# Out-projection by seven block products, with the fox gates last and the GLA output grouped by rows

## The chip, the cores and the metric

One core of one Trainium2 chip. The kernel's time is the device time in microseconds (us) of one launch; a time that is given is the median of several runs. Engines: TensorE (PE in the profile) multiplies matrices, VectorE (DVE), ScalarE (ACT) and GpSimd (POOL) work on elements, SyncE (SP) only issues transfers (DMAs). Each engine runs its own queue in order, and semaphores hold an instruction until what it needs is there.

## The reference

One layer of a decoder trunk over 16 meta tokens and 512 tokens, width D = 2048, in float32. Three token mixers run on disjoint heads of 128: gated DeltaNet (6 heads), GLA (5), forgetting attention, here "fox" (5). Together they give the 16 x 128 = 2048 columns of `o`. Cut to what matters:

```python
proj = rms_norm(x, norm_w) @ w_in                          # all projections, 8 k columns
o_dn  = gated_head_norm(gated_delta_rule_chunked(...), dz, dn_norm_w)   # norm, then * silu(dz)
o_gla = gated_head_norm(gla_chunked(...), gz, gla_norm_w)
o_fox = forgetting_attention(...) * silu(fz)
o = concatenate([o_dn, o_gla, o_fox], -1)[:, PAD:]         # 512 x 2048
out = rms_norm(x + o @ w_out, final_norm_w)                # w_out: 2048 x 2048
```

In one GLA chunk the output is `o = (q*exp(g)) @ S + attn @ v`, and in fox it is `softmax(q @ k.T + c_t - c_s) @ v`.

## The kernel before

**Precision.** A float32 operand of a large product is split into `hi` (a copy on ScalarE in TensorE's fp32r format) and `lo` (the rest, a subtract on VectorE); a product is three matmuls, hi x hi, hi x lo and lo x hi (`split`, L144/L145).

**Stages.** Activations lie with channels on the 128 partitions and tokens along the row. `inproj` (its matmuls are L168, tiles `pp`) makes one block of 128 projected channels from 16 k-blocks x 3 terms = 48 matmuls over 512 tokens; blocks are numbered, and pp42, 46, 50, 54 and 58 are the five fox gates `fz`. Weights come in halves of 512 KB (`load_half`). The order of work is DeltaNet in two groups of three heads, the GLA gates, three GLA pairs (`gla_pair`, two heads of 64 key rows each in one tile), five fox heads (`fox_head`), the out-projection. A planner orders the instructions of each engine from the order of the program, its own costs of instructions, and priorities; weight splits stand in a block of high priority.

**Gates.** `gate_z` projects a gate block, multiplies it by the row norm on VectorE (L299), and `silu` builds z / (1 + exp(-z)) by one GpSimd maximum (L287), three ScalarE functions (L288 and the two lines after it) and one VectorE multiply. For DeltaNet and GLA the gate lies in a tile of the pool `zp` (11 tiles) and the head's output is multiplied into it. In `fox_head` the gate is made inside the head, ahead of its softmax, and the output product `pfo` is multiplied by it when it leaves PSUM.

**GLA output.** L769 adds the attention part, a matmul over 128 rows, and L770 the state part over 64 rows: one head of a pair is in rows 0 to 63 and the other in 64 to 127. The two lines alternate, block after block and head after head.

**Out-projection.** `split_o` splits the 16 head outputs (L905/L906). For each of four 512-wide column chunks, four PSUM banks `pa` (four groups of 128 tokens) gather k-blocks 0 to 13, 3 terms each (L913, in `mms`). Chunks 0 to 2 are then added to the tokens (L949). K-blocks 14 and 15 (LAST = 14) are held back for the end: their weights `wl` are split early, and at the end one tile `pz` after another is made from them (L913) and added (L972), squared with a sum (L974), and multiplied by the norm weight on GpSimd (L976). When a group of tokens has its four chunks, the norm is taken (L978 to L980), the tiles are scaled (L984, L986, L988) and written (L990). The matmuls of chunk 0 need the heads that are done, not the last fox head, so the planner puts them between the steps of that head.

PSUM has eight banks: four of `psb` (projections, `pa`) and four of `psm`. A ring of seven rows of 531 elements (`row`) serves gates, softmax rows, and squares.

Of the kernel before, what the change touches and what calls it, by code (L numbers as in the profile page):

```python
# [8 lines left out]
F32 = mybir.dt.float32  # L9
# [9 lines left out]
P = 128  # L19
# [58 lines left out]
def tile_hybrid_trunk(ctx, tc, xT, xtok, mtok, w_gate, w_in, w_out, consts, lmask, fin_w, out, dbg=None):  # L78
# [5 lines left out]
    hp = pool("hp", 2 * KT)  # L84
    wp = pool("wp", 2)
    zp = pool("zp", 11)
    six = pool("six", 8)
    wk = pool("wk", 2)
# [4 lines left out]
    def row(name, dt=F32):  # L93
        return wk.tile([P, 3 + T], dt, tag="row", bufs=7, name=name)
# [198 lines left out]
    zs = {}  # L293

    def gate_z(kind, h, t=None):
        parts = inproj((kind, h), meta=False)
        p_, t0, n = parts[0]
        z = row(f"z{kind}{h}")[:, :T]
        V.tensor_tensor(out=z[:, :S], in0=p_, in1=rstd[:, t0 : t0 + n], op=ALU.mult)  # L299
# [339 lines left out]
    def gla_pair(p):  # L639
# [125 lines left out]
        for e in range(ne):  # L765
            rr = slice(64 * e, 64 * e + 64)
            for b in range(NB):
                bs = slice(b * P, (b + 1) * P)
                PE.matmul(po[e][:, bs], at[:, e * NB + b, :], vt[:, e, bs], start=True, stop=False)  # L769
                PE.matmul(po[e][:, bs], qd[rr, bs], ss[b][rr, :], start=False, stop=True)  # L770
# [17 lines left out]
    def fox_head(h):  # L788
# [22 lines left out]
        cc = six.tile([P, 2 * T + S], F32, tag="six", name=f"fc{h}")  # L811
        z = wk.tile([P, S], F32, tag="gd", name=f"fz{h}") if h < 2 else cc[:, T + S : T + 2 * S]
        gate_z("fz", h, z)
# [53 lines left out]
        V.tensor_tensor(out=z, in0=po[:, :512], in1=z, op=ALU.mult)  # L867


    for g in range(2):  # L870
        for h in range(max(NF, H * g), H * g + H):
            gate_z("dz", h)
        st = dn_keys(g)
        dn_values(g, st)
        dn_queries(g, st)
        dn_inverse(g, st)
        dn_mix(g, st)
    for h in range(GLA_HEADS):
        gate_z("gz", h)
# [8 lines left out]
    for p in range(3):  # L888
        gla_pair(p)
    for h in range(GLA_HEADS):  # L890
        dump(f"ogl{h}", zs["gz", h])
    for h in range(FOX_HEADS):
        fox_head(h)
    for h in range(FOX_HEADS):
        dump(f"ofx{h}", zs["fz", h])


    heads = [("dz", h) for h in range(DN_HEADS)] + [("gz", h) for h in range(GLA_HEADS)] \
        + [("fz", h) for h in range(FOX_HEADS)]
    oparts = []  # L900

    def split_o(i):
        z = zs[heads[i]]
        hi, lo = part(f"oh{i}"), part(f"ol{i}")
        A.copy(hi, z)  # L905
        V.tensor_tensor(out=lo, in0=z, in1=hi.bitcast(F32), op=ALU.subtract)  # L906
        oparts.append((hi, lo))

    def mms(p_, hi, lo, i, tb, first, last):
        s = slice(tb * P, (tb + 1) * P)  # L910
        oh, ol = oparts[i]
        for n, (o_, w_) in enumerate(((oh, hi), (oh, lo), (ol, hi))):
            PE.matmul(p_, o_[:, s], w_, start=(first and n == 0), stop=(last and n == 2))  # L913

    LAST = 14
    halves = lambda w: [[t[:, j * 512 : (j + 1) * 512] for t in w] for j in range(2)]
    acc, wl = {}, {}

    def load_last(c):
        raw = wp.tile([P, 1024], F32, tag="raw", name=f"rawl{c}")  # L920
        nc.sync.dma_start(out=raw, in_=w_out[c, LAST // 2])
        r = []
        for j in range(2):
            hi, lo = part(f"wlh{c}{j}"), part(f"wll{c}{j}")
            split(raw[:, j * 512 : (j + 1) * 512], hi, lo)
            r.append((hi, lo))
        return r

    for i in range(LAST):
        split_o(i)  # L930
    for cc in range(4):
        pa = [psb.tile([P, 512], F32, tag="b", name=f"pa{cc}{tb}") for tb in range(4)]
        for kp in range(LAST // 2):
            w = halves(load_half(w_out[cc, kp], f"o{cc}_{kp}"))
            for j in range(2):
                i = 2 * kp + j
                for tb in range(4):
                    mms(pa[tb], *w[j], i, tb, i == 0, cc < 3 and i == LAST - 1)
            if cc == 3 and kp % 2 and kp < 6:
                c = kp // 2  # L940
                wl[c] = load_last(c)
        for tb in range(4):
            if 4 * cc + tb < 11:
                a = zp.tile([P, S], F32, tag="zs", name=f"acc{cc}{tb}")
            else:
                a = six.tile([P, S], F32, tag="six", name=f"acc{cc}{tb}")
            nc.scalar.dma_start(out=a, in_=xtok[tb * P : (tb + 1) * P, cc * 512 : (cc + 1) * 512])
            if cc < 3:
                V.tensor_tensor(out=a, in0=a, in1=pa[tb], op=ALU.add)  # L949
            acc[tb, cc] = a  # L950
        if cc == 0:
            for i in range(LAST, KT):
                split_o(i)
    wl[3] = halves(load_half(w_out[3, LAST // 2], "l3"))
    fw = []
    for c in range(4):
        f = part(f"fw{c}").bitcast(F32)
        nc.scalar.dma_start(out=f, in_=fin_w[c * 512 : (c + 1) * 512].partition_broadcast(P))
        fw.append(f)
    ss = wk.tile([P, 4, 5], F32, tag="fss", bufs=1, name="fss")  # L960
    rr = wk.tile([P, 4], F32, tag="frs", bufs=1, name="frs")
    for tb in range(4):
        for cc in (3, 0, 1, 2):
            a = acc[tb, cc]
            cuts = 2 if (tb, cc) == (3, 2) else 1
            for n in range(cuts):
                c = slice(512 // cuts * n, 512 // cuts * (n + 1))
                p_ = pa[tb] if cc == 3 else psm.tile([P, 512], F32, tag="m", name=f"pz{tb}{cc}{n}")
                for j in range(2):
                    hi, lo = wl[cc][j]  # L970
                    mms(p_[:, c], hi[:, c], lo[:, c], LAST + j, tb, cc < 3 and j == 0, j == 1)
                V.tensor_tensor(out=a[:, c], in0=a[:, c], in1=p_[:, c], op=ALU.add)  # L972
                sq = row(f"sqf{tb}{cc}{n}")
                A.activation(sq[:, c], a[:, c], AF.Square, accum_out=ss[:, tb, cc + 2 * n : cc + 2 * n + 1])  # L974
            if cc != 2:
                G.tensor_tensor(out=a, in0=a, in1=fw[cc], op=ALU.mult)  # L976
        r = rr[:, tb : tb + 1]
        V.reduce_sum(r, ss[:, tb, : 3 + cuts], axis=mybir.AxisListType.X)  # L978
        A.activation(r, r, AF.Ln, scale=1.0 / D, bias=eps_c)
        A.activation(r, r, AF.Exp, scale=-0.5)  # L980
        for cc in (3, 0, 1, 2):
            a = acc[tb, cc]
            if cc == 0:
                A.activation(a, a, AF.Copy, scale=r)  # L984
            elif cc == 2:
                V.scalar_tensor_tensor(out=a, in0=a, scalar=r, in1=fw[cc], op0=ALU.mult, op1=ALU.mult)  # L986
            else:
                V.tensor_scalar_mul(a, a, r)  # L988
            q = nc.scalar if cc % 2 else nc.sync
            q.dma_start(out=out[tb * P : (tb + 1) * P, cc * 512 : (cc + 1) * 512], in_=a)  # L990
# [55 lines left out]
```

## Time and profile before

| what | value |
|---|---|
| median of 3 runs | 1048.95 us (1047.97 to 1050.61) |
| profiled execution | 1048.64 us, span 1046.9 us |
| mean granted TensorE clock | 0.991 |
| busy: PE, DVE, ACT, POOL | 1019.8, 574.8, 410.7, 134.9 us |
| L168, three groups of 1456 matmuls | 378.5, 376.8, 376.2 us |
| L913, three groups of 224 matmuls | 88.0, 87.9, 79.1 us |
| bytes moved | 105.15 MB, mean 100 GB/s |

A group row of the profile reads: line, engine, operation, output and input tiles, shapes, count, then busy time, mean ns of one, and the idle time before it with what ended that. Busy times of matmuls overlap in the pipeline, so the time of one is read from a window: its length over its count. A timeline row has start and length in us, then the same names; in brackets stands the wait ahead of it.

### The profile page before, as it was taken

Reading aid. Unit: us, or ns where it says so; the run is one execution under the profiler, and the core shown is the slowest. Engines: PE = TensorE matmul, PEld = TensorE weight load, DVE = VectorE, ACT = ScalarE, POOL = GpSimd, SP = SyncE. Lnnn points to the kernel's source line nnn. Section 1 sums busy time; section 2 is a strip of 40 time slices with the busy share of each in tenths; the row PEclk is TensorE's granted clock in tenths of the full one; section 3 lists DMA queues with packets and bytes.
Section 4 is the critical chain, followed back from the end, with each engine's and each line's share of the span. In section 5 each row is a group of like instructions: output and inputs, shape, how many; then the busy total and the mean of one; then the engine's idle time right before and its main releaser. Section 6 shows DMA issues by size and latency. Waiting matters only on the chain.

```text
span 1046.9 us, 19027 instructions
## 1 busy us (share of the span) xinstructions
PE 1019.8 (97%) x7787; PEld 914.5 (87%) x7787; DVE 574.8 (55%) x1251; ACT 410.7 (39%) x895; POOL 134.9 (13%) x137
## 2 busy tenths in 40 slices
PE   9999999999999999999999999999999999999994
PEld 7899999989999888899989878898989888888883
DVE  6366868855567972334828274455444474332437
ACT  6643533343455333244344443333323262222234
POOL 0021312220213131000100010110101010000014
PEclk9999999999999998999999999999999999999998
DMA  9613222223222322222212122222222263222424
GB/s 351 233 48 127 82 89 92 99 77 108 89 69 82 96 102 77 69 77 73 78 42 67 46 87 74 94 72 86 89 84 87 86 204 126 93 82 100 141 81 160
DMA packets 42347, 105.15 MB, mean 100 GB/s; under 512 B 10589, under 2 KB 13917, under 8 KB 42260
## 3 DMA queue, kind: packets, MB, share of 16 engines
q1 hardware_dynamic: 26848, 90.23, 24.6%
q10 hardware_dynamic: 15412, 13.70, 4.5%
q8 instruction: 61, 1.00, 0.4%
q14 instruction: 26, 0.21, 0.1%
HBM read 98.74 MB, written 5.05 MB: 99 GB/s over the span
## 4 chain that ended last, share of the span: by engine, by line
PE 54%; DVE 3%; ACT 1%; issue 1%; DMA 0%; DVEq 0%
PE pp L168 29%; PE pa L913 15%; PE pss L708 1%; PE pgo L770 1%; PE pfo L863 1%; PE pgo L769 1%; PE pfa L831 1%; PE pz L913 1%; DVE acc L988 1%; PE pfx L846 1%; ACT sqf L974 0%; PE pfd L832 0%; PE pfo L866 0%; DVE acc L986 0%; PE pgk L660 0%
## 5 line engine op out<-in xcount | busy, mean ns | idle before, releaser
L168 PE MATMUL pp<-xh,whi 128*128 128x264 f32 (+2 forms) x1456 | 378.5, 312 | 0.9 <-DVE vg L278 0.8
L168 PE MATMUL pp<-xh,wlo 128*128 128x264 f32 (+2 forms) x1456 | 376.8, 311 | 0.0
L168 PE MATMUL pp<-xl,whi 128*128 128x264 f32 (+2 forms) x1456 | 376.2, 310 | 0.0
L168 PEld LDWEIGHTS pp<-xh,whi 128*128 128x128 f32 x1456 | 244.5, 190 | 16.0 <-issue 1.4
L168 PEld LDWEIGHTS pp<-xl,whi 128*128 128x128 f32 x1456 | 245.2, 190 | 14.4 <-issue 1.4
L168 PEld LDWEIGHTS pp<-xh,wlo 128*128 128x128 f32 x1456 | 245.4, 190 | 13.3 <-issue 0.3
L145 DVE TENSOR_TENSOR wlo<-raw,whi 128x1024 fp32r<-128x1024 f32 x110 | 136.4, 1240 | 124.6 <-ACT whi L144 123.8
L144 ACT CAST whi<-raw 128x1024 fp32r<-128x1024 f32 x110 | 115.3, 1049 | 202.2 <-PE pp L168 181.1
L913 PE MATMUL pa<-whio,ol 128*128 128x512 f32 x224 | 88.0, 393 | 0.0
L913 PE MATMUL pa<-wloo,oh 128*128 128x512 f32 x224 | 87.9, 393 | 0.0
L913 PE MATMUL pa<-whio,oh 128*128 128x512 f32 x224 | 79.1, 396 | 0.0
L145 DVE TENSOR_TENSOR wloo<-rawo,whio 128x1024 fp32r<-128x1024 f32 x28 | 34.6, 1236 | 75.2 <-ACT whio L144 75.1
L144 ACT CAST whio<-rawo 128x1024 fp32r<-128x1024 f32 x28 | 29.4, 1049 | 93.7 <-PE pa L913 60.1
L913 PEld LDWEIGHTS pa<-whio,ol 128*128 128x128 f32 x224 | 42.1, 188 | 9.9
L913 PEld LDWEIGHTS pa<-wloo,oh 128*128 128x128 f32 x224 | 42.1, 188 | 9.5
L913 PEld LDWEIGHTS pa<-whio,oh 128*128 128x128 f32 x224 | 42.0, 188 | 9.2
L287 POOL TENSOR_SCALAR stc<-cv 128x528 f32<-128x528 f32 (+1 forms) x18 | 28.3, 1572 | 165.3 <-DVE cv L361 142.5
L361 DVE SCALAR_TENSOR_TENSOR cv<-pb,cpk,cv 128x528 f32<-128x528 f32 (+1 forms) x54 | 40.8, 755 | 0.6
L976 POOL TENSOR_TENSOR acc<-acc,fw 128x512 f32<-128x512 f32 x12 | 15.7, 1335 | 170.9 <-ACT sqf L974 170.9
L278 DVE TENSOR_TENSOR pb<-pp,rstd 128x264 f32<-128x264 f32 (+1 forms) x36 | 13.8, 424 | 26.2 <-PE pp L168 26.1
L456 DVE TENSOR_TENSOR ot<-ab 51x30 f32<-51x30 f32 (+14 forms) x60 | 20.3, 339 | 3.3 <-POOL stc L287 1.7
L458 DVE TENSOR_TENSOR ab<-ab,ot 51x30 f32<-51x30 f32 (+14 forms) x60 | 20.6, 343 | 1.5
(380 smaller groups left out, 1304.2 us busy)
## 6 DMA issues: line engine op xcount, KB each, us to landing
raw<-in_w_in SPq DMA_DIRECT2D x110, 512.0 KB, 3.2
rawo<-in_w_out SPq DMA_DIRECT2D x28, 512.0 KB, 3.2
xt<-in_xtok SPq DMA_DIRECT2D x8, 512.0 KB, 9.1
acc<-in_xtok ACTq DMA_DIRECT2D x16, 256.0 KB, 5.4
xs<-in_xT SPq DMA_DIRECT2D x7, 528.0 KB, 6.8
rawl<-in_w_out SPq DMA_DIRECT2D x4, 512.0 KB, 5.2
out<-acc SPq DMA_DIRECT2D x8, 256.0 KB, 2.5
out<-acc ACTq DMA_DIRECT2D x8, 256.0 KB, 2.6
```

The source lines that it names most:

```text
L144: A.copy(hi, raw)
L145: V.tensor_tensor(out=lo, in0=raw, in1=hi.bitcast(F32), op=ALU.subtract)
L168: PE.matmul(p_[:, :nt], wt[:, j * m : (j + 1) * m], xx[k][:, t0 : t0 + nt], start=(k == 0 and wt is hi and xx is xh), stop=(k == KT - 1 an ...
L278: V.tensor_tensor(out=o, in0=p_[rows], in1=rstd[rows, t0 : t0 + n], op=ALU.mult)
L287: G.tensor_scalar_max(t, src, LOW)
L361: V.scalar_tensor_tensor(out=c, in0=pb[:, t0 + w : w + T], scalar=cwc[:, blk, w : w + 1], in1=c, op0=ALU.mult, op1=ALU.add)
L456: V.tensor_tensor(out=t3, in0=a3[:, j + 1 :, j : j + 1].to_broadcast([NN * 4 + H, m, j]), in1=a3[:, j : j + 1, 0:j].to_broadcast([NN * 4 + ...
L458: V.tensor_tensor(out=a3[:, j + 1 :, 0:j], in0=a3[:, j + 1 :, 0:j], in1=t3, op=ALU.add)
L708: PE.matmul(ps[o0 : o0 + n, b * n : b * n + n], kx[rr, k0 : k0 + n], qx[rr, q0 : q0 + n], start=True, stop=True)
L769: PE.matmul(po[e][:, bs], at[:, e * NB + b, :], vt[:, e, bs], start=True, stop=False)
L913: PE.matmul(p_, o_[:, s], w_, start=(first and n == 0), stop=(last and n == 2))
L976: G.tensor_tensor(out=a, in0=a, in1=fw[cc], op=ALU.mult)
```

## The change

1. **GLA output.** First all 128-row matmuls of the pair, then the 64-row ones, block by block, the two heads (two row halves) in turn.
2. **Fox gates last.** `fox_head` leaves its ungated output in a `zp` tile by a ScalarE copy; after the fifth head, `gate_z` makes each gate and multiplies it in on VectorE. The planner of the new kernel puts pp42, 46, 50 and 54 inside the last fox heads, where they fill the four `psb` banks, and pp58 after the last output product.
3. **Spills.** The 11 DeltaNet and GLA outputs are written to DRAM (`spill`) and read back, most of them twice, through the ring of rows.
4. **Out-projection by 2 x 2 blocks.** Tokens are cut in two halves of 256 (x1., x2.), the 16 k-blocks in two of 8, and columns into two pairs of chunks (ca, cb). Seven products replace eight. Their token operands are n11 = -x11, n1, t2, x22, n3, x21, n4, sums and differences of four blocks, each split into hi and lo by `put` on 128x256 pieces (56 copies, 56 subtracts). Their weight operands are chunks of w_out or sums of 2, 3 or 4 chunks. A sum is made by loading one chunk (SyncE) and adding others to it by transfers issued on GpSimd (`add_w`, 64 of them, 256 KB each). Each chunk of 128x512 is split on its own, 112 in all. A product is 8 chunks x 2 token groups x 3 terms = 48 matmuls of 128x512.
5. **Memory.** The pools `hp` and `wp` are closed after the last gate and `wk` and `six` after the last head; operands and weight chunks take their room.
6. **End.** The tokens' groups 2 and 3 are finished before the last two products of the second pair; the last product's weights are split ahead; the last of its two token groups is made in two column halves.

The diff, cut to its core (the deleted out-projection is described above):

```diff
+    rw = pool("rw", 1, side="right")
+    early, late = ExitStack(), ExitStack()
+    hp = late.enter_context(tc.tile_pool(name="hp", bufs=2 * KT))
+    wp = late.enter_context(tc.tile_pool(name="wp", bufs=2))
+    wk = early.enter_context(tc.tile_pool(name="wk", bufs=2, side="right"))
+    six = early.enter_context(tc.tile_pool(name="six", bufs=8, side="right"))
...
+    def spill(i):
+        nc.sync.dma_start(out=od[i], in_=zs[heads[i]])
+    def gate_z(kind, h, o=None):
         parts = inproj((kind, h), meta=False)
         p_, t0, n = parts[0]
         z = row(f"z{kind}{h}")[:, :T]
         V.tensor_tensor(out=z[:, :S], in0=p_, in1=rstd[:, t0 : t0 + n], op=ALU.mult)
-        if t is None:
-            t = zp.tile([P, S], F32, tag="zs", name=f"zs{kind}{h}")
-        silu(t, z[:, :S], f"{kind}{h}")
-        zs[kind, h] = t
+        if o is None:
+            o = zs[kind, h] = zp.tile([P, S], F32, tag="zs", name=f"zs{kind}{h}")
+            silu(o, z[:, :S], f"{kind}{h}")
+        else:
+            silu(z[:, :S], z[:, :S], f"{kind}{h}")
+            V.tensor_tensor(out=o, in0=o, in1=z[:, :S], op=ALU.mult)
...
-            rr = slice(64 * e, 64 * e + 64)
             for b in range(NB):
                 bs = slice(b * P, (b + 1) * P)
-                PE.matmul(po[e][:, bs], at[:, e * NB + b, :], vt[:, e, bs], start=True, stop=False)
-                PE.matmul(po[e][:, bs], qd[rr, bs], ss[b][rr, :], start=False, stop=True)
+                PE.matmul(po[e][:, bs], at[:, e * NB + b, :], vt[:, e, bs], start=b == 0, stop=False,
+                          skip_group_check=True)
+        for b in range(NB):
+            bs = slice(b * P, (b + 1) * P)
+            for e in range(ne):
+                rr = slice(64 * e, 64 * e + 64)
+                PE.matmul(po[e][:, bs], qd[rr, bs], ss[b][rr, :], start=False, stop=b == NB - 1,
+                          skip_group_check=True)
...
-        gate_z("fz", h, z)
...
-        V.tensor_tensor(out=z, in0=po[:, :512], in1=z, op=ALU.mult)
+        o = zs["fz", h] = zp.tile([P, S], F32, tag="zs", name=f"of{h}")
+        A.copy(o, po[:, :512])
...
+    KP, HS = KT // 2, S // 2
+    early.close()
+    tp1 = pool("tp1", 6, side="right", reuse_waits="tile")
+    srp = pool("srp", KP, side="right", reuse_waits="tile")
...
+    def put(op, i, src, sign=1.0):
+        hi, lo = (t[:, i] for t in op)
+        if sign > 0:
+            A.copy(hi, src)
+            V.tensor_tensor(out=lo, in0=src, in1=hi.bitcast(F32), op=ALU.subtract)
+        else:
+            A.activation(hi, src, AF.Copy, scale=sign)
+            V.scalar_tensor_tensor(out=lo, in0=src, scalar=sign, in1=hi.bitcast(F32), op0=ALU.mult, op1=ALU.subtract)
...
+    n11, n1, t2 = (operand(tp1, n) for n in ("n11", "n1", "t2"))
+    for i in range(KP):
+        a, b = load_o(i, "oa")
+        put(n11, i, a, -1.0)
+        put(n1, i, sub(f"d1_{i}", a, b))
+    def put_t2(i):
+        a, b = load_o(i, "ob")
+        c, d = load_o(KP + i, "oc")
+        u = sub(f"d2_{i}", a, b)
+        V.tensor_tensor(out=u, in0=u, in1=d, op=ALU.add)
+        put(t2, i, u)
+    for i in range(3):
+        put_t2(i)
+    for h in range(FOX_HEADS):
+        gate_z("fz", h, zs["fz", h])
+        put_t2(h + 3)
...
+    late.close()
+    tp2 = pool("tp2", 8, reuse_waits="tile")
+    wq = pool("wq", 5, reuse_waits="tile")
+    x22, n3, x21, n4 = (operand(tp2, n) for n in ("x22", "n3", "x21", "n4"))
+    for i in range(KP):
+        a, b = load_o(i, "od")
+        c, d = load_o(KP + i, "oe")
+        put(x22, i, d)
+        put(n3, i, sub(f"d3_{i}", b, d))
+        put(x21, i, c)
+        u = sub(f"d4_{i}", c, d)
+        v = sub(f"d5_{i}", a, b)
+        V.tensor_tensor(out=u, in0=u, in1=v, op=ALU.subtract)
+        put(n4, i, u)
...
+    def add_w(t, c, i, name):
+        with tc.high_priority(offset=1000000):
+            nc.gpsimd.dma_start(out=t, in_=w_of(c, i), accum_op=ALU.add)
+    def split_w(raw, name):
+        hi = wq.tile([P, 512], F32R, tag="hi", name=f"{name}h")
+        lo = wq.tile([P, 512], F32R, tag="lo", bufs=4, name=f"{name}l")
+        split(raw, hi, lo)
+        return hi, lo
...
+        def product(ps, op, chunk, first, last):
+            for i in range(KP):
+                made.append(0)
+                w = split_w(chunk(i), f"ws{len(made)}")
+                for tb in range(2):
+                    mms(ps[tb], op, w, i, tb, first and i == 0, last and i == KP - 1)
+        sums = {}
+        def s1(i):
+            t = sums[i] = srp.tile([P, 512], F32, tag="s", name=f"s{pr}{i}")
+            nc.sync.dma_start(out=t, in_=w_of(cb, i))
+            add_w(t, cb, KP + i, f"r1{pr}")
+            return t
+        def s2(i):
+            add_w(sums[i], ca, i, f"r2{pr}")
+            return sums[i]
+        def s4(i):
+            add_w(sums[i], ca, KP + i, f"r4{pr}")
+            return sums[i]
+        def s3(i):
+            t = load_w(ca, i, f"r5{pr}")
+            add_w(t, cb, i, f"r3{pr}")
+            return t
+        y = big("py", *((psb, "b") if pr == 0 else (psm, "m")))
+        z = big("pz", psb, "b")
+        product(y, n11, lambda i: load_w(ca, i, f"w1{pr}"), True, False)
+        for tb in range(2):
+            new_acc(tb, ca)
+            add(tb, ca, y[tb], ALU.subtract)
+        product(z, n1, s1, True, False)
+        if pr == 1:
+            f = tp1.tile([P, KP * HS], F32R, tag="t", name="fw").bitcast(F32)
+            nc.scalar.dma_start(out=f, in_=fin_w.partition_broadcast(P))
+            fw += [f[:, c * 512 : (c + 1) * 512] for c in range(4)]
+        for tb in range(2):
+            new_acc(tb + 2, cb)
+            add(tb + 2, cb, z[tb], ALU.subtract)
+        product(y, t2, s2, False, False)
+        for tb in range(2):
+            new_acc(tb + 2, ca)
+            add(tb + 2, ca, y[tb], ALU.subtract)
+        product(z, x22, s4, False, True)
+        for tb in range(2):
+            add(tb + 2, ca, z[tb])
+            square(tb + 2, ca)
+        product(y, n3, s3, False, False)
+        for tb in range(2):
+            add(tb + 2, cb, y[tb])
+            square(tb + 2, cb)
+        if pr == 1:
+            for tb in (2, 3):
+                for c in (0, 1, 2):
+                    times_fw(tb, c)
+                final(tb, 3)
+            wl = [(tp1 if n < 3 else tp2).tile([P, KP * HS], F32R, tag="t", name=f"wl{n}") for n in range(4)]
+            last_w = []
+            for i in range(KP):
+                raw = load_w(cb, KP + i, "wl")
+                sl = slice(i % 4 * 512, i % 4 * 512 + 512)
+                last_w.append((wl[i // 4][:, sl], wl[2 + i // 4][:, sl]))
+                split(raw, *last_w[-1])
+        w_ = big("pw", psm, "m")
+        product(w_, x21, lambda i: load_w(ca, KP + i, f"w2{pr}"), True, True)
+        for tb in range(2):
+            add(tb, ca, w_[tb])
+            square(tb, ca)
+            new_acc(tb, cb)
+        if pr == 0:
+            product(y, n4, lambda i: load_w(cb, KP + i, f"w4{pr}"), False, True)
+            for tb in range(2):
+                add(tb, cb, y[tb])
+                square(tb, cb)
+        else:
+            for tb in range(2):
+                for c in (0, 1, 2):
+                    times_fw(tb, c)
+                cuts = 1 + tb
+                for n in range(cuts):
+                    cs = slice(512 // cuts * n, 512 // cuts * (n + 1))
+                    for i in range(KP):
+                        mms(y[tb], n4, last_w[i], i, tb, False, n == cuts - 1 and i == KP - 1, cs)
+                    add(tb, cb, y[tb], cs=cs)
+                    square(tb, cb, cb + n, cs)
+                final(tb, 3, 3 + cuts)
```

More of the change, by code (lines that the diff above doesn't have):

```diff
@@ L877, in tile_hybrid_trunk @@
         dn_mix(g, st)
+        for h in range(H * g, H * g + H):
+            spill(h)
     for h in range(GLA_HEADS):
@@ L889, in tile_hybrid_trunk @@
         gla_pair(p)
+        for h in range(2 * p, min(2 * p + 2, GLA_HEADS)):
+            spill(DN_HEADS + h)
     for h in range(GLA_HEADS):
@@ L915, in tile_hybrid_trunk @@
[L915 to L976, printed above, removed]
@@ new lines, in mms @@
+    def mms(p_, op, w, i, tb, first, last, cs=slice(0, 512)):
+        s = slice(tb * P, (tb + 1) * P)
+        (oh, ol), (wh, wl) = op, w
+        for n, (o_, w_) in enumerate(((oh, wh), (oh, wl), (ol, wh))):
+            PE.matmul(p_[:, cs], o_[:, i, s], w_[:, cs], start=first and n == 0, stop=last and n == 2,
+                      skip_group_check=True)
+    ss = rw.tile([P, 4, 5], F32, tag="fss", name="fss")
+    rr = rw.tile([P, 4], F32, tag="frs", name="frs")
+    acc, fw, more, made = {}, [], [], []
```

85 lines of the change are left out of this document (56 added, 29 removed).

## The prediction

> **What bounds the kernel now.** I read the page first (engine shares, the 40 slices, the chain of work), then the windows of the stretches that the change touches, then groups of instructions by shape, and last the timeline at the seams.
>
> ```profile
> span 1046.9 us, 19027 instructions
> PE 1019.8 (97%) x7787; PEld 914.5 (87%) x7787; DVE 574.8 (55%) x1251; ACT 410.7 (39%) x895; POOL 134.9 (13%) x137
> PEclk9999999999999998999999999999999999999998
> GB/s 351 233 48 127 82 89 92 99 77 108 89 69 82 96 102 77 69 77 73 78 42 67 46 87 74 94 72 86 89 84 87 86 204 126 93 82 100 141 81 160
> PE 54%; DVE 3%; ACT 1%; issue 1%; DMA 0%; DVEq 0%
> ```
>
> TensorE works in 97% of the span and carries nearly all of the chain; VectorE is busy in half of it and the transfers in less. So a matmul that goes shortens the kernel by its full time, as long as the other engines stay ahead of it. The profiled execution took 1048.64 us, 1.7 us more than its span; the median of the three runs is 1048.95 us. I sum against 1048.64; the 0.3 us between them is below the 0.3% (3 us) that a measurement of this kernel can tell from no change.
>
> ```profile
> core 0: us, PE busy (x) PEld busy (x) DVE busy (x) ACT busy (x) POOL busy (x), PEclk, DMA share, GB/s
> 0.00:50.00 50.00, 47.63 (x205) 38.66 (x206) 25.53 (x41) 34.52 (x59) 1.86 (x16) 1.00 0.80 296
> 760.00:849.40 89.40, 89.40 (x545) 79.39 (x544) 45.05 (x102) 33.71 (x63) 4.99 (x9) 1.00 0.30 101
> 900.00:983.00 83.00, 83.00 (x361) 67.48 (x360) 26.07 (x27) 17.40 (x18) 0.00 (x0) 1.00 0.29 100
> 1014.00:1034.00 20.00, 19.36 (x89) 15.44 (x87) 15.46 (x21) 10.49 (x33) 11.77 (x9) 1.00 0.29 106
> 1034.00:1046.90 12.90, 0.00 (x0) 0.00 (x0) 6.39 (x11) 4.52 (x15) 3.94 (x4) 0.68 0.47 163
> ```
>
> In the out-projection (900 to 983) TensorE has no gap, VectorE is busy 31% and transfers 29%. That is the room the change spends. The last row is a tail without matmuls.
>
> **Matmuls taken away: -22.1 us.** One 128x512 matmul there is 83.00/361 = 0.2299 us. Before has 16 blocks x 4 row groups x 4 column chunks x 3 terms = 768 of them; after has 2 column pairs x 7 products x 8 chunks x 2 row groups x 3 = 672. 96 x 0.2299 = 22.1 us. The last 24 are cut in two halves, as before's last 6 are; I leave that at nothing.
>
> **GLA output: -6.5 us.** Before alternates, two by two, matmuls over all 128 rows of the array and matmuls over 64.
>
> ```profile
> L769 PE MATMUL pgo<-gvt,kq 128*128 128x128 f32 x40 | 9.5, 318 | 0.0
> 536.12 0.49 PE L769 MATMUL pgo<-gvt,kq 128*128 128x128 f32 x2
> 536.54 0.48 PE L770 MATMUL pgo<-gsn,gqd 64*128 64x128 f32 x2
> 536.96 0.49 PE L769 MATMUL pgo<-gvt,kq 128*128 128x128 f32 x2
> 639.88 0.87 PE L759 MATMUL pgn<-gvt,kdt 128*64 128x128 f32 x6
> ```
>
> Such a group of four takes 536.96 - 536.12 = 0.84 us; forty L769 matmuls make 20 groups, 16.8 us. Six matmuls of the same width that do not alternate take 0.87 us, 0.145 each. Grouped, 80 x 0.145 = 11.6 us bounds the new time from above; if the 64-row ones of the two row halves run at once, 40 x 0.145 + 20 x 0.145 = 8.7 us. The gain lies between 5.2 and 8.1; I take 6.5. The Trainium skill says the same of this edit (TensorEngine Tiling (Array Packing), Key Properties): changing the tiling mode drains TensorE, and different tiles can work in parallel; the 0.84 against 4 x 0.145 = 0.58 agrees with the first half, no row here with the second.
>
> **Tail: -5.1 us.** Before, VectorE is behind when the matmuls end.
>
> ```profile
> 1033.51 0.28 PE L913 MATMUL pz<-wlh,ol 128*128 128x256 f32 x1
> 1037.71 1.33 DVE L972 TENSOR_TENSOR acc<-acc,pz 128x512 f32<-128x512 f32 x3
> L686 DVE TENSOR_TENSOR gdd<-gqk 128x256 f32<-128x256 f32 x14 | 5.8, 418 | 0.1
> L299 DVE TENSOR_TENSOR zfz<-pp,rstd 128x512 f32<-128x512 f32 x5 | 3.4, 689 | 4.5 <-PE pp L168 4.5
> ```
>
> The last add ends at 1039.04, 5.25 us after the last matmul's end (1033.79); from there squares, root, scaling and the output take 7.86 us to 1046.9. After, a product of 8 chunks stands between any two groups of adds, three rows of tokens are finished early, and the last half-tile's add (128x256, 0.418) can follow its matmul. 0.42 + 7.86 = 8.3 us against 13.1; with the 0.3 us by which the last matmuls waited, -5.1.
>
> **Fox head without filler: +5.2 us.** Before, matmuls of the first column chunk run while the last fox head's softmax does. After, the out-projection can't start before the operands are made, and four gate projections (pp42, 46, 50, 54), all that the four banks hold, are used up earlier; the last eight matmuls of pp54 stand in block 2.
>
> ```profile
> 877.74 0.84 PE L831 MATMUL pfa<-fqk 128*128 128x400 f32 x2
> 882.84 0.48 DVE L843 TENSOR_SCALAR fp<-fp,fsm 128x512 f32<-128x512 f32 x1
> ```
>
> From pfa's end (878.58) to the transposes 882.84 + 0.48 = 883.32 is 4.74 us of VectorE and ScalarE work. Block 2 has 8 x 0.2299 = 1.84 us of cover and block 3's first products, about 1.8: 1.1 idle. Block 3 has only block 2's transposes, about 1.6: 3.1 idle. The output product waits about 1 for its low part. 5.2; between 0 and 2 x 4.74 + 1 = 10.5.
>
> **The seam before the first product: +23.1 us.** This is the dearest part. From the last fox product (S0) VectorE has to do, in its queue's order: 30 operations of 128x256 (differences and low parts of n11, n1, the start of t2), then zfz0, the eviction of the first gate; pp58, the fifth gate's 48 matmuls, waits for that bank. Behind it come 12 more gate operations of 128x512 and 13 of 128x256 before the low part of the first weight chunk. The 30 need spilled heads back: 14 reloads, and on the same engines 8 loads of sums, 8 accumulating ones and 6 token tiles, each 256 KB.
>
> ```profile
> 985.58 1.29 DVE L145 TENSOR_TENSOR wll<-rawl,wlh 128x512 fp32r<-128x512 f32 x2
> L287 POOL TENSOR_SCALAR stfz<-zfz 128x512 f32<-128x512 f32 x5 | 7.8, 1565 | 69.0 <-DVE zfz L299 69.0
> acc<-in_xtok ACTq DMA_DIRECT2D x16, 256.0 KB, 5.4
> out<-acc SPq DMA_DIRECT2D x8, 256.0 KB, 2.5
> ```
>
> VectorE alone: 30 x 0.418 = 12.5 us to zfz0. Transfers alone: 36 less about 7 that start before S0 is 29, at 262144 B/296 GB/s = 0.886 us (the rate held over the first 50 us) 25.7 us. Seven row slots serve reloads, differences and gates together, so a reload waits for VectorE to leave a slot, and VectorE 2.5 to 5.4 us for it: I take 19, the middle. zfz0 adds 0.69, then pp58 runs 48 x 0.2299 = 11.0 us. Meanwhile VectorE needs 12 x 0.689 + 13 x 0.418 + 0.69 = 14.4 us: 3.4 uncovered. 19 + 0.7 + 3.4 = 23.1 us without a matmul. ScalarE's 3 x 0.63 and GpSimd's 1.57 a gate fit behind VectorE's. Lower bound: two back-to-back operations take 1.29 us, so one costs 0.60, and a 128x256 one in that proportion 0.364: 43 x 0.364 + 14 x 0.60 - 11.0 = 13.1. Upper: 25.7 + 4.1 = 29.8.
>
> **VectorE inside the first five products: +4.5 us.** x22, n3, x21 and n4 are built while products 1 to 5 run. By the order of instructions VectorE has 10 operations of 128x512 (splits, adds) and 14, 18, 13, 12 and 11 of 128x256 in them: at 0.689 and 0.418, 12.7, 14.4, 12.3, 11.9 and 11.5 us against 11.03 of TensorE, 7.7 over; at 0.60 and 0.364, 1.6 over. I take the middle. Later products have 10 and no excess, but one of the second pair has 20 (13.8 us, 2.8 over, if they fall badly).
>
> **Accumulating transfers: +3.4 us.** No row shows one. The first pair moves 11 reloads, 40 weight chunks, 32 accumulates and 8 token tiles in 7 x 11.03 = 77.2 us: 91 x 0.886 = 80.6 us at 296 GB/s, 3.4 over, if an accumulate costs what a load costs; 91 x 0.747 = 68.0 at the 351 GB/s of the first slice, nothing. I take the first, by the longer stretch. The second pair (84) fits. On GpSimd they stand in one queue with the gates' maximum (L287, before the first five) and eight of the multiplications by the norm weight (L976); about 32 in 44 us leave 1.38 us for each.
>
> **Clock: +1.4 us.** The tail shows a granted 0.68 in 12.9 us without matmuls, so TensorE comes back slower from the 19 us gap. Bounds 0 and 12.9 x 0.32 = 4.1; a third. The Trainium skill (TensorE: Matmul & The Clock Gate, Part 1) has half the rate after one idle window of about 3.4 us and full rate after a busy one; an estimate by that page is 1.7 us a restart, 3.4 for the two.
>
> The spills cost SyncE 11 issues whose data is due when they stand; 0. The fox output is now copied on ScalarE and multiplied later: counted above.
>
> Sum: -22.1 - 6.5 - 5.1 + 5.2 + 23.1 + 4.5 + 3.4 + 1.4 = +3.9; 1048.64 + 3.9 = 1052.5 us.
>
> **Rivals.** *The helpers keep up.* Reloads land ahead, VectorE runs at its back-to-back spacing, transfers at 351 GB/s: seam 13.1, excess 1.6, transfers and clock 0. -22.1 - 6.5 - 5.1 + 5.2 + 13.1 + 1.6 = -13.8: 1034.8 us. For it: VectorE's groups above run without idle, and the first slice moves 351 GB/s. Against it: seven slots, each released only by VectorE. It decides when zfz0 comes within about 16 us of S0 (below that the sum is under zero by 3).
> *An accumulate costs two transfers.* Its destination must be read as well as written. Then pair one moves 123 x 0.747 = 91.9 us against 77.2 (+14.7), pair two 113 x 0.747 = 84.4 (+7.2), the seam 8 more (+6.0); VectorE's 4.5 hides under it: 1052.5 - 3.4 - 4.5 + 27.9 = 1072.5. No row of before speaks for or against. The Trainium skill (DMA: Bandwidth & Descriptors, Rules for kernel authors) says that an accumulate reads its destination and writes it later; what that costs in rate it doesn't say.
> *GpSimd's queue is the bound.* If an accumulate holds it for 1.57 us, like its other instructions here, 32 take 50 against 44: +6; at 2 us +20. About 1062.
>
> **Chances.** Forecast 0.41 (own range 1046 to 1060: within 0.3% 0.13, slower 0.28). Helpers keep up 0.37: the matmuls taken away are certain and the seam is my own sum. Two transfers 0.16, GpSimd 0.06. So faster 0.37, same 0.13, slower 0.50. The range 1034 to 1070 leaves out about a third of the first rival and half of the second, 2 in 10.
>
> **What would show it.** 672 out-projection matmuls near 0.23 us each; GLA output products at 8.7 to 11.6 us in all; a stretch without matmuls before pp58 (about 19 us) and after it (3 to 5) whose releaser is VectorE and behind it a reload; VectorE above 90% in products 2 to 5; a tail near 8 us. Wrong if the seam is under 14 us, or if weight splits wait for accumulating transfers.

## The result, and the profile after

The changed kernel takes 1114.02 us (median of 4 runs, 1109.23 to 1114.10) against 1048.66 us of the kernel before: by the means of the runs 1.0609 times as long, 95% interval 1.0577 to 1.064. Faster was given 0.37, slower 0.50; the forecast of 1052.5 us and the range to 1070 us were far too low.

The page of the changed kernel:

```profile
span 1112.4 us, 19659 instructions
PE 1012.3 (91%) x7709; PEld 905.8 (81%) x7709; DVE 639.9 (58%) x1424; ACT 455.8 (41%) x1017; POOL 189.6 (17%) x201
PEclk9999999999999999999999989999997599889888
GB/s 357 193 58 122 70 94 103 110 91 69 91 90 106 95 92 65 72 105 65 83 59 104 60 77 77 85 86 77 86 94 97 254 200 223 283 204 221 136 213 156
q1 hardware_dynamic: 39664, 105.18, 27.5%
q0 software_dynamic: 9216, 16.78, 8.5%
PE 43%; DMA 9%; DVE 5%; ACT 2%; issue 1%; POOL 0%; ACTq 0%; DVEq 0%; SPq 0%; POOLq 0%
```

TensorE is at 91% instead of 97%; its idle time grew from 27 to 100 us. 62 of the 73 us more lie behind the last fox product, in the last quarter of the span, where the transfers run mostly above 200 GB/s. The row q0 is the queue of the accumulating transfers, and transfers now carry 9% of the chain, where they carried none. The windows, cut at the first fox product, the end of the last, the first product of the new out-projection, and its last matmul:

```profile
core 0: us, PE busy (x) PEld busy (x) DVE busy (x) ACT busy (x) POOL busy (x), PEclk, DMA share, GB/s
0.00:645.70 645.70, 631.14 (x5781) 586.74 (x5782) 392.14 (x882) 281.18 (x657) 101.49 (x100) 0.99 0.30 103
645.70:854.20 208.50, 198.93 (x1187) 175.75 (x1185) 92.28 (x260) 63.73 (x131) 8.89 (x20) 0.97 0.23 77
854.20:904.30 50.10, 13.34 (x51) 10.18 (x49) 24.87 (x56) 18.05 (x41) 14.69 (x13) 0.66 0.79 230
904.30:1104.00 199.70, 168.67 (x696) 133.13 (x696) 128.47 (x222) 91.08 (x185) 64.50 (x69) 0.91 0.82 208
1104.00:1112.40 8.40, 0.25 (x3) 0.04 (x1) 2.12 (x5) 1.73 (x5) 0.00 (x0) 0.64 0.54 188
```

Before, the first fox product stood at 657.4 us, so this point comes 11.7 us earlier. From there to the last matmul before had 376.4 us, 176.6 of them (768 x 0.2299) out-projection; the rest, 199.8, has 11.0 us of pp58 in it. So the stages changed like this:

| stage | before | after | change | forecast |
|---|---|---|---|---|
| to the first fox product | 657.4 | 645.7 | -11.7 | -6.5 |
| fox heads without pp58 | 188.8 | 208.5 | +19.7 | +5.2 |
| seam with pp58 | 11.0 | 50.1 | +39.1 | +23.1 |
| out-projection | 176.6 | 199.7 | +23.1 | -22.1 + 7.9 |
| tail | 13.1 | 8.4 | -4.7 | -5.1 |

(The forecast's 1.4 us for the clock lie across the stages.) The changes add to 65.5 us, which is the difference of the spans. 672 matmuls at 0.2299 us are 154.5 us: the seven products lose 45.2 us, the seam 39.1. Of the 45.2 us, TensorE is idle for 31.0 (199.70 - 168.67). The trace's record of the granted clock has 37.5 us at half speed in the products, and matmuls run in 20.8 of them, which loses another 10.4 us. The waits of TensorE in this part, by what released it:

```profile
PE pp L171 <- DVE zfz L308: 33.3, 1, 33.3
PE py L1007 <- DVE ws73l L148: 8.3, 1, 8.3
PE py L1007 <- ACT ws38h L147: 8.3, 1, 8.3
PE py L1007 <- DVE acc L1027: 7.7, 1, 7.7
PE pfx L860 <- DVE fp L857: 7.2, 2, 3.8
PE py L1007 <- ACT ws1h L147: 3.4, 1, 3.4
```

The columns are us in total, times, longest. The largest wait is the one that the prediction named, the bank that zfz0 frees, but 33 us instead of 19. What VectorE waited for in it, from its groups by shape:

```profile
L945 DVE TENSOR_TENSOR d<-oa 128x256 f32<-128x256 f32 x8 | 3.4, 423 | 20.5 <-DMA oa<-od 19.9 <-PE pfo L877 0.6
```

19.9 us for reloads. It is the reloads that set this wait, not VectorE's own 12.5 us of work.

### The profile page after: what moved, and what is told of

The parts are those of the page before. It is cut to its first block, busy times and chain, and to the rows that moved or that the text cites. A ratio compares the mean times of both kernels' runs of the same rounds, so it can differ in the third digit from the quotient of the medians.

```text
span 1112.4 us, 19659 instructions
## 1 busy us (share of the span) xinstructions
PE 1012.3 (91%) x7709; PEld 905.8 (81%) x7709; DVE 639.9 (58%) x1424; ACT 455.8 (41%) x1017; POOL 189.6 (17%) x201
## 4 chain that ended last, share of the span: by engine, by line
PE 43%; DMA 9%; DVE 5%; ACT 2%; issue 1%; POOL 0%; ACTq 0%; DVEq 0%; SPq 0%; POOLq 0%
PE pp L171 26%; PE py L1007 6%; DMA r<-in_w_out 3%; PE pw L1007 2%; DMA s<-in_w_out 2%; DMA acc<-in_xtok 2%; PE pz L1007 1%; PE pss L719 1%; DMA oa<-od 1%; PE pfo L877 1%; DVE ws73l L148 1%; PE pfa L845 1%; PE pfx L860 1%; DMA oe<-od 1%; DMA wl<-in_w_out 1%
## 5 line engine op out<-in xcount | busy, mean ns | idle before, releaser
L995 POOL DMA_DIRECT2D s<-in_w_out x48 | 43.4, 1183 | 86.8 <-DVE n11l L933 43.2
L995 POOL DMA_DIRECT2D r<-in_w_out x16 | 13.8, 865 | 70.4 <-DMA r<-in_w_out 49.4
L863 ACT CAST fphi<-pfx 128x384 fp32r<-128x384 f32 (+2 forms) x20 | 8.0, 398 | 38.2 <-PE pfx L860 38.2
L290 POOL TENSOR_SCALAR stdz<-zdz 128x512 f32<-128x512 f32 x6 | 11.2, 1872 | 65.7 <-DVE zdz L308 65.7
L849 DVE CUSTOM_DVE_ANT_0 fp<-pfa,fc 128x16 f32<-128x16 f32 (+3 forms) x20 | 7.4, 369 | 26.0 <-PE pfa L845 26.0
L854 ACT ACTIVATE fp<-fp,fsm 128x144 f32<-128x144 f32 (+3 forms) x20 | 11.5, 575 | 24.7 <-DVE fsm L853 22.3
L837 POOL CAST ptmhi<-zero_c 128x512 fp32r<-128x512 f32 x5 | 3.1, 610 | 105.7 <-PE pfo L877 105.7
L740 POOL TENSOR_TENSOR gkd<-gkd,gqk 128x512 f32<-128x512 f32 (+1 forms) x3 | 9.0, 2988 | 68.6 <-ACT gkd L739 68.6
L584 POOL TENSOR_TENSOR eg<-eg,qT 128x384 f32<-128x384 f32 x8 | 8.4, 1050 | 69.2 <-DVE egl L583 38.6
```

The costliest lines, as they stand in the source:

```text
L290: G.tensor_scalar_max(t, src, LOW)
L854: A.activation(pr[:, : m + P], pr[:, : m + P], AF.Exp, bias=sm[:, 2:3], accum_out=sm[:, 3:4])
L995: nc.gpsimd.dma_start(out=t, in_=w_of(c, i), accum_op=ALU.add)
```

## The experiments

All ratios are to the kernel before in runs of the same chip.

**e1: the accumulating transfers as plain ones**

```diff
-            nc.gpsimd.dma_start(out=t, in_=w_of(c, i), accum_op=ALU.add)
+            nc.gpsimd.dma_start(out=t, in_=w_of(c, i))
```

> The changed kernel with its 64 accumulating transfers as plain ones: same queue, bytes, waits and order of every instruction; they overwrite the sum instead of adding to it, so the sums of weights are left out. Theory RATE (an accumulate holds the transfer engines about twice as long as a load: by the changed kernel's queue rows 8.5% for 16.78 MB against 27.5% for 105.18 MB, 1.94 per byte, and that starves reloads and weight sums): 64 x 0.72 us of transfer time go, the seam loses 5 to 10 us and the products 20 to 30, about 1080 us. Theory ORDER (not the adding but the number of transfers and their place in the queues makes the waits): 1105 to 1114 us.

1089.82 us, ratio 1.0396 (1.0372 to 1.042): 24 us less by the medians (in the trace, 3.5 in the seam and 18.6 in the products). The expectation of 1080 was 10 too low, but RATE holds and ORDER does not. Two things changed with the adding: the plain transfers went in 4096 packets of 4 KB instead of 8192 of 2 KB (beside 1024 of 4 bytes in both), and each held GpSimd for less time (544 ns instead of 1183, mean of 48). The packet size is not the cause: in the trace of the changed kernel a plain 2 KB packet of a load took 84 ns (median) and an accumulating one 178, and in e1 a plain one of 4 KB took 159. The shorter issue was not tested alone; GpSimd is busy for 64.5 of the 199.7 us of products.

**e2: no adding transfers**

```diff
-            nc.gpsimd.dma_start(out=t, in_=w_of(c, i), accum_op=ALU.add)
+            pass
```

> The changed kernel without the 64 accumulating transfers at all (the weight sums are left out; the products then use the chunk that SyncE loaded). RATE: a little below the kernel with plain transfers, 1065 to 1075 us; what is left is the seam's VectorE work, the uncovered fox steps and the clock. ORDER: the 64 transfers and their GpSimd issues are gone, so it falls as far, but then the kernel with plain transfers stays near 1110. If neither moves, the reloads and VectorE alone make the waits: above 1100 us.

1066.89 us, ratio 1.0183 (1.0157 to 1.0209): 23 us less again. The queue row in the page of e1; then the seam and the products in the windows of e1, and of e2:

```profile
q0 software_dynamic: 5120, 16.78, 4.4%
```

```profile
852.20:898.80 46.60, 13.41 (x50) 10.16 (x48) 24.85 (x55) 18.09 (x41) 12.08 (x13) 0.67 0.73 247
898.80:1079.90 181.10, 165.28 (x696) 132.81 (x696) 126.42 (x222) 91.30 (x185) 48.26 (x69) 0.94 0.68 230
```

```profile
853.00:893.30 40.30, 14.44 (x50) 10.95 (x48) 23.37 (x53) 17.67 (x39) 6.85 (x5) 0.66 0.68 226
893.30:1060.20 166.90, 159.59 (x695) 129.12 (x696) 127.87 (x225) 91.82 (x186) 19.43 (x13) 0.98 0.50 163
```

The last columns but one give the time of the 16 transfer engines: share times length, seam and products together, is 203.3 us in the changed kernel (50.1 x 0.79 + 199.7 x 0.82), 157.2 in e1, 110.9 in e2. The steps are 46.1 and 46.3 us, 0.72 us for each of 64 transfers. So 256 KB take 0.72 us, and adding them to what lies in SBUF takes 1.44: two transfers. The queue rows say nearly the same: 8.5% of 1112.4 us is 1.48 us a transfer, 4.4% of 1088.3 is 0.75. It agrees with the Trainium skill (DMA: Bandwidth & Descriptors, Rules for kernel authors), by which an accumulate reads its destination and writes it later. In the changed kernel, while products 2 to 5 of the first pair run, the transfer engines are full by these records, at a share of 1.03:

```profile
915.30:982.00 66.70, 52.12 (x199) 39.14 (x198) 45.21 (x98) 27.43 (x57) 26.11 (x30) 0.87 1.03 240
```

**e3: the fox gates in the heads again**

```diff
+        gate_z("fz", h)
...
-        o = zs["fz", h] = zp.tile([P, S], F32, tag="zs", name=f"of{h}")
-        A.copy(o, po[:, :512])
+        o = zs["fz", h]
+        V.tensor_tensor(out=o, in0=po[:, :512], in1=o, op=ALU.mult)
...
     for h in range(FOX_HEADS):
-        gate_z("fz", h, zs["fz", h])
         put_t2(h + 3)
```

> The changed kernel with the fox gates made inside the heads as before (the rest as changed). Theory COVER (taking the gates out of the heads uncovers their softmax steps, 9.6 us idle and about 7 us at half clock in the trace, and puts five gate chains into the seam): 1114 - 16 in the heads - about 10 in the seam (the gates' VectorE operations go, pp58's 11 us of matmuls go with them from the seam into the heads) = about 1088 us. Rival: the seam is set by reloads and the cover of pp58 is lost there: 1100 to 1108 us.

1111.01 us, ratio 1.06 (1.0542 to 1.0658). COVER as I had put it is false, and the rival's 1100 to 1108 us was missed too. The windows of e3 (heads, seam, products):

```profile
648.00:863.80 215.80, 203.70 (x1228) 180.60 (x1226) 100.83 (x272) 70.74 (x146) 15.51 (x26) 0.95 0.24 79
863.80:867.30 3.50, 0.42 (x3) 0.04 (x1) 2.55 (x7) 1.93 (x6) 0.00 (x0) 0.98 0.91 277
867.30:1095.70 228.40, 183.99 (x696) 138.13 (x696) 134.81 (x257) 95.11 (x198) 73.03 (x76) 0.87 0.87 221
```

The seam is gone (3.5 us), and the products take 28.7 us more: the same transfers are now crowded there, at a share of 0.87 (seam and products together 201.9 us of all 16 engines, against 203.3). And the heads gain little: 215.8 us with 41 projection matmuls more (9.4 us) than in the 208.5, so 2.1 us; TensorE is still idle in them for 12.1 us (215.80 - 203.70).

**e4: the kernel before with the GLA grouping alone** (the first hunk of the change's `gla_pair`)

> The kernel before with the GLA output grouping alone. By the changed kernel's trace (the stage from the first GLA projection to the first fox product took 145.6 us against 157.9) it saves about 11 us: 1037.5 us. By the prediction's term 6.5 us: 1042. If the planner's order of the fillers made the stage shorter and not the grouping: 1046 to 1049.

1040.35 us, ratio 0.9919 (0.9895 to 0.9943): 8.7 us faster than the kernel before, the best of all that ran. The attention part and most of the state part of the GLA output, in the groups of e4:

```profile
L768 PE MATMUL pgo<-gvt,kq 128*128 128x128 f32 x40 | 4.9, 275 | 0.0
L774 PE MATMUL pgo<-gsn,gqd 64*128 64x128 f32 x30 | 2.5, 272 | 0.0
```

Busy time of the first group fell from 9.5 to 4.9 us, of the second from 7.3 to 2.5. In the changed kernel's timeline 16 of the one and 16 of the other take 1.87 and 1.10 us, from start to start:

```profile
535.75 1.95 PE L779 MATMUL pgo<-gvt,kq 128*128 128x128 f32 x16
537.62 0.49 PE L785 MATMUL pgo<-gs,gqd 64*128 64x128 f32 x4
537.95 0.84 PE L785 MATMUL pgo<-gsn,gqd 64*128 64x128 f32 x12
538.72 0.39 PE L171 MATMUL pp<-xh,whi 128*128 128x264 f32 x1
```

That is 0.069 us for a 64-row matmul against 0.117 for a 128-row one of the same width: the two row halves do overlap. For all 80 matmuls these times make 7.4 us instead of 16.8, 9.4 less, close to what e4 gained.

**e5: the first sums held back**

```diff
+            if pr == 0:
+                G.tensor_copy(t[:, 0:1], zs["fz", 0][:, 0:1])
             nc.sync.dma_start(out=t, in_=w_of(cb, i))
```

> The changed kernel with the first pair's eight weight sums held back: a one-column copy on GpSimd from the first gated fox tile stands before each sum's load, so that neither the loads nor the accumulating transfers run beside the reloads. Theory ORDER (in the seam the reloads wait because sum loads and accumulates stand ahead of them): the seam, 50 us, shrinks by the three waits of VectorE for reloads (8.4 + 5.0 + 4.1) to 33 to 36 us and the kernel comes to about 1098. Theory VOLUME (seam and products together are set by the time of the transfers, 203 us of all 16 engines in 250 us): the seam shrinks and the first products wait for the sums instead, 1108 to 1116 us.

1110.99 us, ratio 1.06 (1.0571 to 1.0628). VectorE's wait for reloads falls from 19.9 to 7.9 us and the seam from 50.1 to 43.4; the products rise from 199.7 to 205.2. That is as VOLUME has it, and ORDER is out. But holding the sums back also makes the sums themselves later, so the run shows that the time moved from the seam into the products, not that no order could save some of it.

**e6: gates in the heads and no adding transfers** (e3 and e2 together)

> Fox gates in the heads and no adding transfers (sums left out). What is left of the change when both the seam's gates and the adding are gone. VOLUME: with 111 us of transfers instead of 203 over 165 us of matmuls nothing waits for them any more, the products take 165 to 172 us, the seam 4 to 10: 648 + 216 + 7 + 168 + 8 = 1047 us. If VectorE's operand work (over 11 us a product) or the row ring is a bound of its own: products 180 to 190 us, 1062 to 1070, no better than the kernel without adds.

1058.46 us, ratio 1.0102 (1.0077 to 1.0127), between the two cases. The seam is 3.7 us, the products 177.8 us against 154.5 of matmuls. So with the adding away altogether the change would still lose to the kernel before, by 1%. Emptying the seam is worth 8.4 us here (e2 to e6); beside the adding it was worth 3.0 (the changed kernel to e3), with intervals that overlap.

**e7: additions on GpSimd instead of accumulating transfers**

```diff
+    gsp = pool("gsp", 3, reuse_waits="tile")
...
-        with tc.high_priority(offset=1000000):
-            nc.gpsimd.dma_start(out=t, in_=w_of(c, i), accum_op=ALU.add)
+        more_w = gsp.tile([P, 512], F32, tag="g", name=f"{name}{i}")
+        nc.sync.dma_start(out=more_w, in_=w_of(c, i))
+        G.tensor_tensor(out=t, in0=t, in1=more_w, op=ALU.add)
```

> The changed kernel with each accumulating transfer replaced by a plain load into a ring of three tiles and an addition on GpSimd (128x512, 1.34 us by the multiplications by the norm weight). VOLUME: the transfers fall by 46 us as in the kernel with plain transfers, but 64 additions are 85 us of GpSimd beside VectorE: between 1085 and 1095 us. If GpSimd's additions and VectorE's subtractions hold each other up, 1100 us and more.

1112.14 us, ratio 1.0623 (1.0595 to 1.0651). The second case: the transfers fall to a share of 0.62 in the products, but VectorE's busy time there rises from 128.5 to 166.5 us for one operation more, and GpSimd's additions take 1.63 us instead of the 1.34 that I reckoned with. The additions also lost the high priority that the transfers had; what that is worth was not tested.

```profile
L997 POOL TENSOR_TENSOR s<-s,r 128x512 f32<-128x512 f32 x48 | 77.6, 1630 | 96.6 <-DMA r<-in_w_out 61.9 <-DVE ws65l L148 15.7 <-DVE ws9l L148 11.2
```

**e8: e4 with the last adds and squares at high priority**

```diff
+                with tc.high_priority(offset=1000000):
                     V.tensor_tensor(out=a[:, c], in0=a[:, c], in1=p_[:, c], op=ALU.add)
...
```

> The kernel before with the GLA grouping, and in its last stage the adds of the last products and the squares in a block of high priority for the planner, so that they stand ahead of the scaling of finished tokens. If VectorE's queue order makes the 5.25 us by which the last add is behind the last matmul: 2 to 4 us less than with the grouping alone, about 1037. If that lateness comes from the operations themselves (a scaling that took 1.78 us beside a GpSimd multiplication): no difference, 1040.

1040.48 us, ratio 0.9935 (0.9915 to 0.9955): no difference to e4. But it decides nothing: in the traces of e4 and e8 VectorE runs the same operations in the same order from start to end, and the scaling of 1.77 us still stands ahead of the last three adds. The planner did not move them, so the queue's order as the cause of the late add stays untested.

**e9: the norm weight on VectorE**

```diff
-        G.tensor_tensor(out=a, in0=a, in1=fw[c], op=ALU.mult)
...
-            if c == last:
+            if True:
                 V.scalar_tensor_tensor(out=a, in0=a, scalar=r, in1=fw[c], op0=ALU.mult, op1=ALU.mult)
```

> The changed kernel without the GpSimd multiplications by the norm weight: the last scaling of every tile multiplies by row factor and norm weight in one VectorE operation. Theory LOCK (in the second pair eight such multiplications in a row, 10.15 us, hold a VectorE subtraction of 0.69 us for 9.06 us, TensorE waits 8.27 us for it and runs 10.2 us at half clock after it): 8.3 + about 5 us go, 1101 us. Rival VOLUME: in that stretch transfers are late anyway and the wait only moves to a sum: 1110 to 1114 us.

1109.9 us, ratio 1.06 (1.0559 to 1.0642). The wait that it aims at, in the timeline of the changed kernel:

```profile
1025.11 10.15 POOL L1036 TENSOR_TENSOR acc<-acc,fw 128x512 f32<-128x512 f32 x8
1026.75 9.06 DVE L148 TENSOR_TENSOR ws73l<-s,ws73h 128x512 fp32r<-128x512 f32 x1 [4.69 <-ACT ws73h L147]
1035.87 0.80 PE L1007 MATMUL py<-ws73l,t2h 128*128 128x512 f32 x1 [8.27 <-DVE ws73l L148]
```

An operation of 0.69 us lasts 9.06 us, until GpSimd's row of eight is done. In e9 the subtraction takes 0.69 us, the wait is gone, and the products take 192.6 us, 7.1 less; the tail grows by 1.0 us, and the median fell by 4.1 us only, with intervals that overlap. So LOCK holds: the multiplications held the subtraction. What that is worth in the time is not settled. The Trainium skill (SBUF — State Buffer, SBUF: two separate sides) calls it an exclusive lock, held for a whole instruction, between GpSimd and a VectorE operation with two SBUF inputs; here the subtraction, which started during the second of the eight, was held until the last had ended.

**e10: e3 and e9 together**

> Fox gates in the heads and the norm weight multiplied on VectorE, accumulating transfers as changed: does the changed out-projection come near the kernel before when its seam is emptied and the GpSimd multiplications are gone? VOLUME: 203 us of transfers in 233 us of seam and products stay, so no more than the 5 to 10 us of the multiplications on top of the gates' 3: 1100 to 1107 us. If waits add up: 1095 us or less.

1104.13 us, ratio 1.0542 (1.051 to 1.0574): as VOLUME has it. The products take 224.9 us at a share of 0.88, which is 198 us of transfers. Against e3 the norm weight is worth 6.9 us here, again with intervals that overlap.

**e11: the kernel before with its out-projection held until the last fox head is done**

```diff
+        if cc == 0:
+            for tb in range(4):
+                PE.matmul(pa[tb][:, :P], zs["fz", 4][:, :P], zs["fz", 4][:, :P], start=True, stop=True)
```

> The kernel before, with its first out-projection matmuls held until the last fox head is done (four small matmuls that read its output start the four banks and are overwritten). Theory COVER by the out-projection: the last head's softmax steps stand uncovered as in the changed kernel (9.6 us idle there, of which 3.8 at the first head, and 6.8 us at half clock after each), so about 6 + 3.4 + the wait for the last head's split (1 to 3): 12 us more than before, 1060 us. If the planner covers it with other work: 1049 to 1052 us.

1070.71 us, ratio 1.0218 (1.0176 to 1.026): 23 us, about twice the 12 that were expected. Its waits of TensorE from the fox heads on:

```profile
PE pfx L846 <- DVE fp L843: 14.2, 4, 6.7
PE pa L935 <- DVE fc L867: 0.8, 1, 0.8
```

There are 15.8 us of idle time with the smaller ones, where 6 were expected. The trace's record of the granted clock has 23.9 us at half speed from 853.1 us on, where before has none; matmuls run in 12.1 of them, which loses some 6 us more. So the out-projection of before was what covered the last fox head. That is the part of COVER that holds, and it fits that putting the gates back (e3) left 12.1 us of idle time in the heads.

## Why the prediction was wrong, step by step

- **Matmuls taken away, -22.1 us:** right as a count. 672 ran (the last 24 as 48 halves); at full clock they are 154.5 us. They took 199.7 us for the reasons below.
- **GLA, -6.5 us:** too small. Alone 8.7 us; in the changed kernel the stage became 11.7 us shorter. My lower end for it, 8.7 us, put 0.145 us on each of the 128-row matmuls; 16 of them took 1.87 us, 0.117 each. Two 64-row ones side by side took 0.137, near the 0.145 of that end. 1.2 us of the 11.7 are matmuls that moved into the next stage.
- **Tail, -5.1 us:** right, -4.7.
- **Fox head, +5.2 us:** mis-sized, +19.7. I counted only the last head. The first head stood uncovered too (3.8 us), the idle time was 9.5 us in all, and each of the two stops goes with 6.8 us at half clock by the trace's clock record. Matmuls ran in 10.9 of these 13.7 us, so 5.4 us were lost, 2.7 a stop. With 1.2 us of matmuls that moved here from the stage before this makes 16.1; 3.6 us of the 19.7 I can't place. e11 shows the mechanism in the kernel before.
- **Accumulating transfers, +3.4 us:** this step failed, and it is the main one. I took the price of a load. The second rival had the mechanism, at 0.16, and e1 and e2 show its size: 1.44 against 0.72 us, worth 24 us here, with another 23 us for the transfers as such, where I had 3.4 us at a load's price. The prediction's own sign of being wrong, a weight split that waits for an accumulating transfer, came true: ws38h waited 8.3 us for the tile `r`. In products 2 to 5 of the first pair the transfer engines were full (the last row under e2). Even so the rival's 1072.5 us was far too low. It had the two pairs 14.7 and 7.2 us over their matmuls; they were 23.0 and 22.3 over (100.2 and 99.5 us). (Its 113 transfers of the second pair should be 116, by the prediction's own 84 and 32: 2.2 us more, which changes nothing.) It took the excess as an average, as if transfers could be made ahead of need. By the program they can't: the sums live in eight tiles of `srp` and five of `wq`, each refilled only after its last use, and what is late shows as single waits (8.3 us for ws38h; 7.7 us for an add that stands behind weight splits whose loads are late). The second pair, with the engines at a share of 0.71, loses by such waits and not by volume. That averaging is the reason is argued from the program and these waits; no run tested it.
- **Seam, +23.1 us:** right in its place and its releaser, outside its bounds in size: 39.1. zfz0 came 32.6 us after the last fox product, where 25.7 was my end. I reckoned with 296 GB/s; the seam moved 230 at a share of 0.79, for the accumulates' bytes count once and take twice. Without the 64 transfers (e2) the seam is 40.3 us, 29.3 without pp58's 11.0, just inside my upper bound of 29.8; so 9.8 of the 16.0 us of the miss are theirs, and the other 6.2 come of a middle that was too low. e5 and e3 show more: what is taken from the seam comes back in the products.
- **VectorE in the products, +4.5 us:** not the bound. I expected VectorE above 90% in products 2 to 5; it is busy 45.2 of the 66.7 us in that row (68%), and 128.5 of 199.7 us in all. Its in-order queue matters where an operation in it waits, for a transfer or for GpSimd (9.06 us).
- **Clock, +1.4 us:** too small. The clock record has 85 us at half speed between 645 and 1104 us, in eight stretches. Matmuls ran in 35 of these, so some 17.6 us were lost (5.4 in the heads, 1.7 in the seam, 10.4 in the products). Every stop of more than 3 us in the waits above is paid again in the matmuls after it: at half clock they follow one another by 0.43 us instead of 0.23. The prediction's rule from the Trainium skill (TensorE: Matmul & The Clock Gate, Part 1) agrees: the stretches are 3.4 us or multiples of it. The estimate by it was 1.7 us a restart; the two stops in the heads cost 2.7 each, and there were eight stretches where I had counted two restarts.
- **GpSimd's queue as the bound:** no. It is busy 64.5 of 199.7 us there.
- **The helpers keep up, 0.37:** excluded by the seam alone.

What stays open: the 12 us by which e2's products, with no adding transfer left, exceed 154.5 us, and e6's 23. By the traces TensorE is idle for 7.3 and 13.4 us of them, and half clock under running matmuls loses 3.0 and 6.2; but which of the waits for operands and accumulator adds would go with what, no run separates.

## What to carry to other kernels

Fewer matmuls pay only while what they are bought with stays under TensorE's time: add up the transfers of the stage in time of the transfer engines, not in bytes, with an accumulating transfer as two, and leave room, since transfers that wait for buffers can't be averaged over a stage. Before work is taken from one place, ask what it covered there; here 191 out-projection matmuls, 44 us of them, stood beside the last attention head (849.4 to 899.5 us). A pause of TensorE of more than 3 us cost its length and, in every case here, the half clock after it.

## What the runs showed of the hardware that I had not expected

- An accumulating transfer from DRAM into SBUF took the 16 transfer engines 1.44 us for 256 KB, a plain one 0.72 (178 against 84 ns for a packet of 2 KB), and its issue held GpSimd longer (1183 ns against 544 in e1, mean of 48).
- Eight GpSimd multiplications in a row held one VectorE subtraction of 0.69 us for 9.06 us.
- Matmuls on the two 64-row halves in turn took about 0.069 us each, 128-row ones of the same width 0.117; before, where they alternated, four took 0.84.
